# Two transformer layers and a scan block on one core: per-head 64-row products from compact operands in the second layer, and five modulation rounds moved from the first feed-forward into it

## The chip, the cores and the metric

The kernel runs on one core of a Trainium2 chip. The metric is the device time of one execution in microseconds (us); lower is better. Three executions of the kernel before gave 3799.74, 3799.99 and 3803.73 us, so the median is 3799.99 us.

## The reference, cut to what matters

512 latent tokens and 256 context tokens of width 1024 pass through two layers and then a third block. Every layer begins with a modulation: six vectors of 1024 values computed from a condition vector, used as shift, scale and gate.

```python
mod = silu(c) @ w_mod[l] + b_mod[l]          # 6 x 1024, for latent and for context
x = x + gate1 * mixer(norm(x) * (1 + scale1) + shift1)
x = x + gate2 * ffn(norm(x) * (1 + scale2) + shift2)
```

Layer 0 mixes by attention. Layer 1 ("odd") mixes by a neighbourhood attention and by a two-directional scan (RWKV-7) over 8 heads of 64:

```python
def step(S, inp):                            # S: 64 x 64 for each head, state of the scan
    sa = einsum('bhvk,bhk->bhv', S, kk_t)
    S = S * w_t - sa[..., None] * (kk_t * a_t) + v_t[..., None] * k_t
    return S, einsum('bhvk,bhk->bhv', S, r_t)
```

The scan runs over the context first, forward and backward; its end states start the scans over the latent tokens. The third block ("layer 2") has its own modulation `mod[2]`.

## The kernel before, in words

Everything is feature-major: 128 features on the partitions, tokens along the row. A large product is three matmuls for each pair of blocks (high and low halves of weights and activations), written by `mm3` (L361). A weight tile of 512 KB comes through a ring of three buffers (tag `wraw`), is rounded by ScalarE (`whi`, L321), and its remainder is taken by GpSimd (`wlo`, L322), each with two buffers.

**Modulation.** `mods(s, bias, rounds, dst)` (L367 to L392) computes one third of the six vectors in each round. A round has 8 steps; each loads two raw tiles of 512 KB (`mraw`, L377) and issues four matmuls of 32 output rows on four column strips (`psmod`, L380; the trace has two instructions for each of these float32 matmuls, so 8 in a step). At the end of a round the row is copied and transposed (`psmt`, L387). The steps are drawn one at a time by a generator, so other code can lay them between its own. In layer 0's feed-forward (`ffn`, called by `layer0`) all six rounds of `wm1` and `wm2` are drawn: 8 steps before the norm and 40 inside the loop over hidden blocks. Their raw tiles use the same ring of three buffers as the weights.

**The scan in chunks of 64.** Phase 1 (`rw_phase1`) computes for each pair of heads j (0 to 3) and direction d the operands of the chunked scan: `mix` makes k, v and r from the projection (`psz`, 24 matmuls each, then GpSimd L869 and VectorE L870, L871), `rw_pair` normalises, and `rw_dir` makes decays `E` and the operands `az` and `BKn`. `az` holds a pair of heads in a zero-padded layout: head e's 64 partitions are filled only in block e, so that a product over 128 rows gives both heads side by side.

```python
s.az = [pi.tile([128, s.nar, 2, n], F32, name=f"az{i}") for i in range(2)]
nc.tensor.matmul(ps[:, c * w:c * w + w], BKn[:, g + c]..., az[:, :, :, (g + c) * 64:(g + c) * 64 + 64])
```

The result `psA` (L1004) is masked by VectorE into `M` (L1006), multiplied with v (L1011) and copied out by ScalarE (L1012); operands go to DRAM. `rw_tri` inverts small triangular blocks on VectorE (`trisolve`, L792 and L794) and writes them to the DRAM tensors `dZ`, `dZT` in 16 transfers (L1041), half from the queue of SyncE (SP), half from that of ScalarE. Phase 2 (`rw_phase2`, `rw_unit`) loads these operands by unit (L1052 to L1066) and runs the chain of the scan.

**Order.** In `layer1` phase 1 of the context runs beside the projections of the neighbourhood attention; then phase 1 of the latent tokens runs with `rw_tri` and phase 2 of the context as its side work; then the neighbourhood attention with `rw_tri` of the latent; then phase 2 of the latent. A scheduler of the framework turns the program order into an order for each engine; each engine and each DMA queue then runs its own list strictly in order.

Of the kernel before, what the change touches and what calls it, by code (L numbers as in the profile page):

```python
# [8 lines left out]
F32 = mybir.dt.float32  # L9
# [3 lines left out]
ALU = mybir.AluOpType  # L13
# [230 lines left out]
class Base:  # L244
# [467 lines left out]
    def layer0(self):  # L712
# [33 lines left out]
        self.side = chain(self.mods(1, "bm1", (0, 1, 2), self.mod[1]), self.mods(2, "bm2", (0, 1, 2), self.mod[2]))  # L746
# [20 lines left out]
class K1:  # L767
# [74 lines left out]
    def rw_phase1(self, s):  # L842
# [4 lines left out]
        with ExitStack() as es:  # L847
# [7 lines left out]
            s.az = [pi.tile([128, s.nar, 2, n], F32, name=f"az{i}") for i in range(2)]  # L855
            s.vu = [pi.tile([128, s.nch, 128], F32, name=f"vu{i}") for i in range(2)]
            for z in s.az + s.vu:
                nc.gpsimd.memset(z, 0.0)
# [89 lines left out]
    def rw_dir(self, s, d, j, tp):  # L948
# [34 lines left out]
        for e in range(2):  # L983
            p = slice(64 * e, 64 * e + 64)
            if s.lat:
                nc.gpsimd.tensor_tensor(ch(az[p, 1, e]), ch(r[p]), E[p, :, i0:i0 + 64], op=ALU.mult)
                nc.sync.dma_start(s.dR[d][p, j], az[p, 1, e])
            nc.vector.tensor_tensor(ch(az[p, 0, e]), ch(kk[p]), E[p, :, iprev:iprev + 64], op=ALU.mult)
            nc.sync.dma_start(s.dAf[d][p, j], az[p, 0, e])
# [5 lines left out]
        w = nar * 128  # L995
        per = 512 // w
        mk = self.b(f"mar{d}")[:, :w].unsqueeze(1).to_broadcast([128, per, w])
        hc = max(per, nch // 2)
        for g in range(0, nch, per):
            if g % hc == 0:  # L1000
                M = tp.tile([128, hc, nar, 2, 64], F32, tag=f"M{d}", name="M", bufs=1)
            ps = s.psv("psA")
            for c in range(per):
                nc.tensor.matmul(ps[:, c * w:c * w + w], BKn[:, g + c].rearrange("p s t -> p (s t)"), az[:, :, :, (g + c) * 64:(g + c) * 64 + 64],  # L1004
                                 start=True, stop=True)
            nc.vector.tensor_tensor(M[:, g % hc:g % hc + per].rearrange("p c s e t -> p c (s e t)"), ps.rearrange("p (c x) -> p c x", c=per), mk, op=ALU.mult)  # L1006
            yield
            for c in range(g, g + per):
                for e in range(2):
                    o = ((c - g) // 2) * 128 + e * 64  # L1010
                    nc.tensor.matmul(ps[64 * (c % 2):64 * (c % 2) + 64, o:o + 64], M[:, c % hc, 0, e], vu[:, c, e * 64:e * 64 + 64], start=True, stop=True)  # L1011
            nc.scalar.activation(t2[:, g * 64:(g + per) * 64], ps[:, :per * 64], AF.Copy)  # L1012
            if (g + per) % hc == 0:
                g0 = g + per - hc
                for c in range(2):
                    nc.sync.dma_start(s.dA[d][:, c, g0 // 2:(g0 + hc) // 2, j].rearrange("p b e t -> p b (e t)"), M[0:64, c::2, 0].rearrange("p b e t -> p b (e t)"))
                if s.lat:
                    nc.sync.dma_start(s.dRR[d][:, j, g0:g0 + hc], M[:, :, 1].rearrange("p c e t -> p c (e t)"))
# [4 lines left out]
            yield  # L1023
        nc.sync.dma_start(s.dBV[d][:, j].rearrange("p b v -> p (b v)"), t2)

    def rw_tri(self, s):
        nc = self.nc
        Lq = 8 * s.nb
        with self.pool(name="tri", bufs=1, side="left") as trp, self.pool(name="trips", bufs=1, space=PSUM, side="right") as tps:
# [7 lines left out]
            for d in range(2):  # L1037
                for z, dst in ((Zs[d], s.dZ[d]), (ZTs[d], s.dZT[d])):
                    for p in range(4):
                        sl = slice(32 * p, 32 * p + 32)  # L1040
                        (nc.sync, nc.scalar)[d].dma_start(dst[sl, :, sl].rearrange("i u j -> u i j"), z[Lq * p:Lq * p + Lq])  # L1041
# [289 lines left out]
    def layer1(self):  # L1331
# [3 lines left out]
        with self.pool(name="psd1a", bufs=2, space=PSUM) as pA, self.pool(name="psd1d", bufs=3, space=PSUM) as pD, self.pool(name="psd1b", bufs=3, space=PSUM) as pB:  # L1335
# [4 lines left out]
            gF = self.gain("nffn1", m, 0, 4, "g1F")  # L1340
# [15 lines left out]
            st_c.side, st_c.bq, st_c.bc, st_c.bl, st_c.bk = "right", 2, 2, 1, 1  # L1356
# [10 lines left out]
        with self.pool(name="psd1c", bufs=2, space=PSUM) as pA, self.pool(name="psd1f", bufs=2, space=PSUM) as pD:  # L1367
# [849 lines left out]
```

## Time and profile before

| | before |
|---|---|
| median of three executions | 3799.99 us (3799.74 to 3803.73) |
| the profiled execution: its own time | 3793.68 us |
| its span from first to last instruction | 3791.9 us |
| TensorE (PE) busy | 3377.0 us (89%) |
| VectorE (DVE) busy | 1701.5 us (45%) |
| GpSimd (POOL) busy | 1402.0 us (37%) |
| ScalarE (ACT) busy | 1308.5 us (35%) |
| mean granted TensorE clock | 0.945 of 2.4 GHz |

Shares over the whole span hide the stages. The stages are read from windows: 515 to 1117 us is layer 0's feed-forward, 1117 to 1265 us phase 1 of the context, 1265 to 1592 us phase 1 of the latent tokens with the context's phase 2 beside it, 1592 to 1707 us the neighbourhood attention, and then the latent's phase 2.

### The profile page before, as it was taken

The numbers are of one execution on the slowest core, as the hardware profiler recorded it, in microseconds if no ns is written. First come the engines' busy times: TensorE is split into PE (matmuls) and PEld (weight loads), VectorE is DVE, ScalarE is ACT, GpSimd is POOL, SyncE is SP. The second block draws the span as 40 slices with busy tenths as digits, with TensorE's granted clock in tenths as the row PEclk, the third lists the DMA queues.
The fourth block names the chain that finished last, engine by engine and source line by source line (L and its number), as shares of the span: only waits on it lengthen the run. The fifth ranks groups of instructions, "written<-read, shape, count | busy, mean of one in ns | idle before, by whom it ended". The sixth has DMA issues, their size and how long they took to land. (4 is left out here: it accounts for less than half of the span.)

```text
span 3791.9 us, 49466 instructions
## 1 busy us (share of the span) xinstructions
PE 3377.0 (89%) x18772; PEld 2652.6 (70%) x18772; DVE 1701.5 (45%) x3170; ACT 1308.5 (35%) x2263; POOL 1402.0 (37%) x940
## 2 busy tenths in 40 slices
PE   7989989999999768888889989997898698789997
PEld 3679868787878546667768877666777457658885
DVE  4566231111124596574554426447657767431112
ACT  3366231121224433332234432333545323232222
POOL 1453222222223453321335544434544343244442
PEclk9999999999999878999889999998999899999999
DMA  6420243434334434636423433433455668512221
GB/s 230 164 106 7 88 151 117 150 116 141 126 106 129 111 111 140 175 88 204 146 70 124 131 105 95 122 93 99 140 155 155 158 193 247 164 61 95 95 97 65
DMA packets 397757, 480.78 MB, mean 127 GB/s; under 512 B 148432, under 2 KB 288656, under 8 KB 396496
## 3 DMA queue, kind: packets, MB, share of 16 engines
q1 hardware_dynamic: 384976, 476.05, 40.6%
q10 hardware_dynamic: 12544, 1.57, 0.3%
q8 instruction: 149, 2.44, 0.3%
q14 instruction: 88, 0.72, 0.1%
HBM read 391.86 MB, written 85.66 MB: 126 GB/s over the span
## 5 line engine op out<-in xcount | busy, mean ns | idle before, releaser
L322 POOL TENSOR_TENSOR wlo<-wraw,whi 128x1024 fp32r<-128x1024 f32 (+2 forms) x371 | 867.1, 2339 | 1512.7 <-ACT whi L321 1345.3
L321 ACT ACTIVATE whi<-wraw 128x1024 fp32r<-128x1024 f32 (+2 forms) x371 | 380.2, 1026 | 1041.3 <-issue 240.8
L504 DVE TENSOR_TENSOR pu<-pu,sg 128x512 f32<-128x512 f32 x88 | 55.6, 632 | 606.9 <-PE pu L361 554.2
L361 PE MATMUL pd<-hidh,wlo 128*128 128x512 f32 (+1 forms) x704 | 262.0, 372 | 9.2 <-POOL wlo L322 8.9
L361 PE MATMUL pd<-hidh,whi 128*128 128x512 f32 (+1 forms) x704 | 263.4, 374 | 6.1 <-ACT whi L321 3.8
L361 PE MATMUL pd<-hidl,whi 128*128 128x512 f32 (+1 forms) x704 | 260.5, 370 | 0.2 <-DVE hidl L506 0.2
L361 PE MATMUL pg<-hil,whi 128*128 128x512 f32 x528 | 214.3, 406 | 28.8 <-ACT hil L449 15.4
L361 PE MATMUL pg<-hil,wlo 128*128 128x512 f32 x528 | 211.4, 400 | 8.1 <-POOL wlo L322 7.1
L361 PE MATMUL pu<-hil,whi 128*128 128x512 f32 x528 | 209.7, 397 | 5.8 <-ACT whi L321 5.8
L361 PE MATMUL pu<-hil,wlo 128*128 128x512 f32 x528 | 209.2, 396 | 6.0 <-POOL wlo L322 6.0
L361 PE MATMUL pg<-lol,whi 128*128 128x512 f32 x528 | 210.5, 399 | 2.5 <-DVE lol L450 2.4
L361 PE MATMUL pu<-lol,whi 128*128 128x512 f32 x528 | 208.9, 396 | 0.0
L361 PE MATMUL psp<-hil,whi 128*128 128x512 f32 x416 | 174.0, 418 | 25.6 <-DVE yo L1782 11.8
L361 PE MATMUL psp<-lol,whi 128*128 128x512 f32 x416 | 171.0, 411 | 2.9 <-DVE lol L450 2.9
L361 PE MATMUL psp<-hil,wlo 128*128 128x512 f32 x416 | 170.3, 409 | 1.9 <-POOL wlo L322 1.8
L513 DVE SCALAR_TENSOR_TENSOR xT<-pd,mod,xT 128x512 f32<-128x512 f32 x80 | 59.8, 749 | 244.6 <-PE pd L361 244.6
L361 PEld LDWEIGHTS pd<-hidh,whi 128*128 128x128 f32 x704 | 133.3, 189 | 46.8 <-issue 15.1
L361 PEld LDWEIGHTS pd<-hidh,wlo 128*128 128x128 f32 x704 | 133.4, 189 | 39.1 <-POOL wlo L322 15.4
L361 PEld LDWEIGHTS pg<-hil,whi 128*128 128x128 f32 x528 | 101.5, 192 | 71.8 <-ACT hil L449 18.6
L361 PEld LDWEIGHTS pd<-hidl,whi 128*128 128x128 f32 x704 | 133.3, 189 | 24.0 <-issue 0.9
L792 DVE TENSOR_TENSOR Tl<-Al,Zl 64x31 f32<-64x31 f32 (+15 forms) x248 | 145.2, 585 | 4.1
L1574 DVE SCALAR_TENSOR_TENSOR psp<-xpl,vecs,psp 128x512 f32<-128x512 f32 x144 | 107.8, 751 | 84.5 <-ACT psp L1570 58.1
(588 smaller groups left out, 8145.9 us busy)
## 6 DMA issues: line engine op xcount, KB each, us to landing
mraw<-in_wm_dram SPq DMA_DIRECT2D x144, 512.0 KB, 4.3
wraw<-in_w2c_dram SPq DMA_DIRECT2D x72, 512.0 KB, 3.3
wraw<-in_wf0in_dram SPq DMA_DIRECT2D x44, 512.0 KB, 3.6
wraw<-in_wf1in_dram SPq DMA_DIRECT2D x44, 512.0 KB, 3.6
Z<-dZ SPq DMA_DIRECT2D x48, 256.0 KB, 3.8
ZT<-dZT SPq DMA_DIRECT2D x48, 256.0 KB, 4.1
wraw<-in_w1d_dram SPq DMA_DIRECT2D x23, 512.0 KB, 3.9
wraw<-in_wf2g_dram SPq DMA_DIRECT2D x22, 512.0 KB, 3.2
```

The source lines that it names most:

```text
L321: self.nc.scalar.activation(hi[:, :nk], t[:, :nk], AF.Copy)
L322: self.nc.gpsimd.tensor_tensor(lo[:, :nk], t[:, :nk], hi[:, :nk].bitcast(F32), op=ALU.subtract)
L361: nc.tensor.matmul(ps, l, r, start=first and i == 0 and p == 0, stop=last and i == n - 1 and p == 2)
L504: nc.vector.tensor_tensor(u, u, sg[:, :n], op=ALU.mult)
L513: nc.vector.scalar_tensor_tensor(x[:, j], pd[:, :n], gv[:, j:j + 1], x[:, j], op0=ALU.mult, op1=ALU.add)
L792: nc.vector.tensor_tensor(tmp, A[:L, rows, t:t + 1].to_broadcast([L, nr, ncl]), Z[:L, t:t + 1, cols].to_broadcast([L, nr, ncl]), op=ALU.mult)
L1574: nc.vector.scalar_tensor_tensor(pv, xp[:, :, t:t + L], w(t), pv, op0=ALU.mult, op1=ALU.add)
```

## The change

Of the six rounds of `wm1` and `wm2`, only the first stays in layer 0's feed-forward. The other five (40 steps) are drawn once per round of `rw_phase1` of the latent tokens, with a PSUM bank and a small pool of their own; what is left is drawn at the end. The gain vector `g1F` is computed later. `az` becomes compact, 128 partitions without zero blocks, filled in one instruction and stored with one transfer where there were two; the product is taken per head over 64 rows into two PSUM banks of four chunks each, and the mask is applied to each. The bank counts change: 2 to 3 for phase 1 of the latent, 2 and 2 to 1 and 1 for phase 2 of the context. The 16 `dZ` transfers all go to SP's queue. Phase 1 gets a further yield per group, and phase 2 of the context is drawn twice per round from round 13 on.

```diff
         self.mpools = self.psd, self.tp, (self.wp, "wraw", 3)
-        self.side = chain(self.mods(1, "bm1", (0, 1, 2), self.mod[1]), self.mods(2, "bm2", (0, 1, 2), self.mod[2]))
+        self.side = self.mods(1, "bm1", (0,), self.mod[1])
...
-            s.az = [pi.tile([128, s.nar, 2, n], F32, name=f"az{i}") for i in range(2)]
+            s.az = [pi.tile([128, s.nar, n], F32, name=f"az{i}") for i in range(2)]
...
-            for z in s.az + s.vu:
+            for z in s.vu:
                 nc.gpsimd.memset(z, 0.0)
...
-        for e in range(2):
-            p = slice(64 * e, 64 * e + 64)
-            if s.lat:
-                nc.gpsimd.tensor_tensor(ch(az[p, 1, e]), ch(r[p]), E[p, :, i0:i0 + 64], op=ALU.mult)
-                nc.sync.dma_start(s.dR[d][p, j], az[p, 1, e])
-            nc.vector.tensor_tensor(ch(az[p, 0, e]), ch(kk[p]), E[p, :, iprev:iprev + 64], op=ALU.mult)
-            nc.sync.dma_start(s.dAf[d][p, j], az[p, 0, e])
+        if s.lat:
+            nc.gpsimd.tensor_tensor(ch(az[:, 1]), ch(r), E[:, :, i0:i0 + 64], op=ALU.mult)
+            nc.sync.dma_start(s.dR[d][:, j], az[:, 1])
+        nc.vector.tensor_tensor(ch(az[:, 0]), ch(kk), E[:, :, iprev:iprev + 64], op=ALU.mult)
+        nc.sync.dma_start(s.dAf[d][:, j], az[:, 0])
...
-        w = nar * 128
-        per = 512 // w
+        w = nar * 64
+        per = 4
...
-            ps = s.psv("psA")
+            pa = [s.psv("psA") for e in range(2)]
             for c in range(per):
-                nc.tensor.matmul(ps[:, c * w:c * w + w], BKn[:, g + c].rearrange("p s t -> p (s t)"), az[:, :, :, (g + c) * 64:(g + c) * 64 + 64],
-                                 start=True, stop=True)
-            nc.vector.tensor_tensor(M[:, g % hc:g % hc + per].rearrange("p c s e t -> p c (s e t)"), ps.rearrange("p (c x) -> p c x", c=per), mk, op=ALU.mult)
+                for e in range(2):
+                    p = slice(64 * e, 64 * e + 64)
+                    nc.tensor.matmul(pa[e][:, c * w:c * w + w], BKn[p, g + c].rearrange("p s t -> p (s t)"), az[p, :, (g + c) * 64:(g + c) * 64 + 64],
+                                     start=True, stop=True)
+            for e in range(2):
+                nc.vector.tensor_tensor(M[:, :, :, e], pa[e][:, :per * w].rearrange("p (c s t) -> p c s t", c=per, t=64), mk, op=ALU.mult)
             yield
+            ps = pa[0]
...
             yield
+            if s.lat:
+                yield
...
-                        (nc.sync, nc.scalar)[d].dma_start(dst[sl, :, sl].rearrange("i u j -> u i j"), z[Lq * p:Lq * p + Lq])
+                        nc.sync.dma_start(dst[sl, :, sl].rearrange("i u j -> u i j"), z[Lq * p:Lq * p + Lq])
...
-            st_c.side, st_c.bq, st_c.bc, st_c.bl, st_c.bk = "right", 2, 2, 1, 1
+            st_c.side, st_c.bq, st_c.bc, st_c.bl, st_c.bk = "right", 1, 1, 1, 1
...
-        with self.pool(name="psd1c", bufs=2, space=PSUM) as pA, self.pool(name="psd1f", bufs=2, space=PSUM) as pD:
+        with self.pool(name="psd1c", bufs=2, space=PSUM) as pA, self.pool(name="psd1f", bufs=3, space=PSUM) as pD, \
+                self.pool(name="psd1m", bufs=1, space=PSUM) as pM, self.pool(name="mrow", bufs=1) as pR:
+            self.mpools = pM, pR, (self.wp, "wraw", 3)
+            mods = chain(self.mods(1, "bm1", (1, 2), m), self.mods(2, "bm2", (0, 1, 2), self.mod[2]))
...
             for i, _ in enumerate(self.rw_phase1(st_l)):
-                self.step(2 if i > 16 and i % 2 else 1)
+                self.step(2 if i > 12 else 1)
+                next(mods, None)
             self.drain()
+            for _ in mods:
+                pass
```

The order of instructions moves in three places. The first is SP's queue in layer 0's feed-forward. Before, every pair of weight loads (`wraw`) has a pair of modulation loads (`mraw`) beside it:

```order
L377 DMA mraw<-in_wm_dram 128x1024 x2
L315 DMA wraw<-in_wf0in_dram 128x1024 x2
L377 DMA mraw<-in_wm_dram 128x1024 x2
L315 DMA wraw<-in_wf0in_dram 128x1024 x2
L377 DMA mraw<-in_wm_dram 128x1024 x2
L315 DMA wraw<-in_wf0out_dram 128x1024
```

Now the weights stand alone there, up to the first loads of layer 1:

```order
L315 DMA wraw<-in_wf0in_dram 128x1024 x16
L315 DMA wraw<-in_wf0out_dram 128x1024 x8
L315 DMA wraw<-in_wf0in_dram 128x1024 x16
L315 DMA wraw<-in_wf0out_dram 128x1024 x8
L315 DMA wraw<-in_wf0in_dram 128x1024 x12
L315 DMA wraw<-in_wf0out_dram 128x768 x8
```

So the feed-forward loses 40 steps, and nothing takes their place. The second place is PE's list in phase 1 of the latent tokens, at the products `psA` of one head pair (j = 0). Before, they stand between projections `psz` of the next pair:

```order
L361 MATMUL psz<-hil,wlo 128x512
L1004 MATMUL psA<-az_10756,BKn 128x256 x2
L1004 MATMUL psA<-az_10757,BKn 128x256 x2
L361 MATMUL psz<-hil,whi 128x512
L361 MATMUL psz<-lol,whi 128x512
L361 MATMUL psz<-hil,wlo 128x512
```

Now they have half the columns, are twice as many, and modulation matmuls stand before and between them:

```order
L361 MATMUL psz<-hil,wlo 128x512
L380 MATMUL psmod<-mraw,siluc 32x512 x4
L1002 MATMUL psA<-az_10420,BKn 128x128
L1002 MATMUL psA<-az_10421,BKn 128x128 x4
L380 MATMUL psmod<-mraw,siluc 32x512 x2
L1011 MATMUL psA<-vu_10422,M 64x64
L380 MATMUL psmod<-mraw,siluc 32x512 x2
L1002 MATMUL psA<-az_10421,BKn 128x128 x4
L1011 MATMUL psA<-vu_10422,M 64x64 x8
L361 MATMUL psz<-hil,whi 128x512
```

The steps moved into gaps that the scheduler saw around `psA`; the 40 steps stand in 58 such rows. The third place is the end of the neighbourhood attention, where `rw_tri` of the latent stores its blocks. On SP's queue before (the other eight stand on ScalarE's):

```order
L1041 DMA dZ_1507<-Zl 32x32x32 x4
L1041 DMA dZT_1509<-Al 32x32x32 x4
L1052 DMA Z<-dZ_1507 128x512
L1294 DMA dno_9442<-no 128x512
L1053 DMA ZT<-dZT_1509 128x512
```

and now:

```order
L1041 DMA dZ_1507<-Zl 32x32x32 x4
L1041 DMA dZT_1509<-Al 32x32x32 x4
L1041 DMA dZ_1508<-Zl 32x32x32 x4
L1041 DMA dZT_1510<-Al 32x32x32 x4
L1294 DMA dno_9068<-no 128x512
L1052 DMA Z<-dZ_1507 128x512
L1053 DMA ZT<-dZT_1509 128x512
```

The first loads of phase 2 now stand behind all 16 stores, and ScalarE's list has none.

## Rows read from the trace of the kernel before

**Rows 1.** Windows by stage: width, busy time of engines (instructions), granted clock, DMA share, GB/s.

```profile
515.00:1117.00 602.00, 597.70 (x3461) 489.22 (x3459) 85.00 (x157) 109.39 (x158) 156.01 (x68) 1.00 0.38 128
1117.00:1265.00 148.00, 127.89 (x787) 107.85 (x788) 77.82 (x131) 77.50 (x139) 60.40 (x43) 0.96 0.41 129
1265.00:1592.00 327.00, 248.13 (x1355) 182.93 (x1356) 222.25 (x386) 111.00 (x190) 131.49 (x93) 0.83 0.47 133
```

**Rows 2.** PE's waits in 515:1117: who waited for whom, total us, times, longest.

```profile
PE pd L361 <- POOL wlo L322: 2.7, 5, 0.8
```

**Rows 3.** Windows, instructions on tile psmod, then psmt: PE, PEld, DVE.

```profile
515.00:1117.00 602.00, 41.55 (x312) 6.14 (x312) 3.46 (x5) 1.00 0.38 128
...
515.00:1117.00 602.00, 2.99 (x20) 2.30 (x20) 1.28 (x10) 1.00 0.38 128
```

**Rows 4.** PE's timeline around one step: start, length, instructions, idle before.

```profile
559.52 1.07 PE L380 MATMUL psmod<-mraw,siluc 128*32 128x512 f32 x8
560.52 0.50 PE L361 MATMUL pg<-hil,whi 128*128 128x512 f32 x1
```

**Rows 5.** PE's waits in 1265:1592, the longest total.

```profile
PE psA L1004 <- DVE BKn L992: 40.7, 7, 11.1
```

**Rows 6.** Timelines of DVE, POOL and PE in one such wait.

```profile
1337.19 0.68 DVE L988 TENSOR_TENSOR az<-kk,E 64x512 f32<-64x512 f32 x1
...
1342.36 2.24 DVE L988 TENSOR_TENSOR az<-kk,E 64x512 f32<-64x512 f32 x1
...
1348.42 2.05 PE L1004 MATMUL psA<-az,BKn 128*128 128x256 f32 x4 [9.90 <-DVE BKn L992]
```

**Rows 7.** Groups by line and shape in 1265:1592: busy us, mean ns.

```profile
L988 DVE TENSOR_TENSOR az<-kk,E 64x512 f32<-64x512 f32 x16 | 19.2, 1199 | 0.2
...
L986 POOL TENSOR_TENSOR az<-r,E 64x512 f32<-64x512 f32 x16 | 24.6, 1538 | 11.3 <-ACT E L976 10.5
...
L858 POOL MEMSET az<- 128x2048 f32 x2 | 3.5, 1805 | 0.0
```

**Rows 8.** PE's timeline at the start of the latent's phase 1.

```profile
1304.16 0.76 PE L361 MATMUL psz<-hil,whi 128*128 128x512 f32 x1 [12.12 <-DVE tw L871]
```

**Rows 9.** ACT's timeline at the end of the context's `rw_tri`.

```profile
1462.73 0.69 ACT L961 ACTIVATE t<-psa,small 128x512 f32<-128x512 f32 x1 [4.91 <-DMA dZT<-Al]
```

**Rows 10.** Timelines of ACT, SP and PE at the end of the latent's `rw_tri`.

```profile
1706.18 0.60 ACT L1276 ACTIVATE ptile<-pt 128x512 f32<-128x512 f32 x1 [9.46 <-DMA dZT<-Al]
...
1692.56 4.00 SPq L1041 DMA_DIRECT2D dZ<-Zl  x4
1696.66 8.31 SPq L1041 DMA_DIRECT2D dZT<-Al  x4
...
1710.45 0.32 SPq L1053 DMA_DIRECT2D ZT<-dZT  x1
...
1713.86 2.04 PE L1070 MATMUL p<-ZT,U 128*128 128x128 f32 x8 [5.06 <-DMA U<-rwl]
```

**Rows 11.** SP's timeline in layer 2, first and last of 16 such stores from one queue.

```profile
2981.80 2.98 SPq L1735 DMA_DIRECT2D dZ<-Zl  x4
...
2992.42 3.74 SPq L1735 DMA_DIRECT2D dZT<-Al  x4
```

**Rows 12.** PE's timeline, 128-column and 256-column float32 products at full clock.

```profile
1558.71 0.61 PE L1123 MATMUL psc<-UV,bk 128*128 128x128 f32 x4
1559.16 1.46 PE L1004 MATMUL psA<-az,BKn 128*128 128x256 f32 x6
```

**Rows 13.** PE's timeline in a unit of the context's phase 2.

```profile
1542.99 0.66 PE L1093 MATMUL p<-Z,at 128*64 128x128 f32 x8 [1.72 <-DVE at L1088]
```

**Rows 14.** Tile mraw in 76:260 (layer 0's projections): idle time that its users spent.

```profile
DMA mraw<-in_wm_dram: 6.7, 4
```

**Rows 15.** SP's timeline, twelve modulation loads in a row through three buffers.

```profile
468.56 24.08 SPq L377 DMA_DIRECT2D mraw<-in_wm_dram  x12
```

**Rows 16.** Windows as in rows 1, one wait for `BKn`.

```profile
1340.00:1360.00 20.00, 3.93 (x8) 2.35 (x8) 19.81 (x23) 2.58 (x4) 16.20 (x9) 0.56 0.41 125
```

More of the change, by code (lines that the diff above doesn't have):

```diff
@@ L993, in rw_dir @@
         yield
-        w = nar * 128
-        per = 512 // w
-        mk = self.b(f"mar{d}")[:, :w].unsqueeze(1).to_broadcast([128, per, w])
-        hc = max(per, nch // 2)
+        w = nar * 64
+        per = 4
+        mk = self.b(f"mar{d}")[:, :2 * w].rearrange("p (s e t) -> p s e t", e=2, t=64)[:, :, 0].unsqueeze(1).to_broadcast([128, per, nar, 64])
         for g in range(0, nch, per):
-            if g % hc == 0:
-                M = tp.tile([128, hc, nar, 2, 64], F32, tag=f"M{d}", name="M", bufs=1)
-            ps = s.psv("psA")
+            M = tp.tile([128, per, nar, 2, 64], F32, tag=f"M{d}", name="M", bufs=1)
+            pa = [s.psv("psA") for e in range(2)]
             for c in range(per):
-                nc.tensor.matmul(ps[:, c * w:c * w + w], BKn[:, g + c].rearrange("p s t -> p (s t)"), az[:, :, :, (g + c) * 64:(g + c) * 64 + 64],
-                                 start=True, stop=True)
-            nc.vector.tensor_tensor(M[:, g % hc:g % hc + per].rearrange("p c s e t -> p c (s e t)"), ps.rearrange("p (c x) -> p c x", c=per), mk, op=ALU.mult)
+                for e in range(2):
[4 more added lines that the diff above has]
+                nc.vector.tensor_tensor(M[:, :, :, e], pa[e][:, :per * w].rearrange("p (c s t) -> p c s t", c=per, t=64), mk, op=ALU.mult)
             yield
+            ps = pa[0]
             for c in range(g, g + per):
@@ L1010, in rw_dir @@
                     o = ((c - g) // 2) * 128 + e * 64
-                    nc.tensor.matmul(ps[64 * (c % 2):64 * (c % 2) + 64, o:o + 64], M[:, c % hc, 0, e], vu[:, c, e * 64:e * 64 + 64], start=True, stop=True)
+                    nc.tensor.matmul(ps[64 * (c % 2):64 * (c % 2) + 64, o:o + 64], M[:, c - g, 0, e], vu[:, c, e * 64:e * 64 + 64], start=True, stop=True)
             nc.scalar.activation(t2[:, g * 64:(g + per) * 64], ps[:, :per * 64], AF.Copy)
[L1013 to L1018, printed above, removed]
+            for c in range(2):
+                nc.sync.dma_start(s.dA[d][:, c, g // 2:(g + per) // 2, j].rearrange("p b e t -> p b (e t)"), M[0:64, c::2, 0].rearrange("p b e t -> p b (e t)"))
+            if s.lat:
+                nc.sync.dma_start(s.dRR[d][:, j, g:g + per], M[:, :, 1].rearrange("p c e t -> p c (e t)"))
             if g == 0:
@@ L1023, in rw_dir @@
             yield
+            if s.lat:
+                yield
         nc.sync.dma_start(s.dBV[d][:, j].rearrange("p b v -> p (b v)"), t2)
@@ L1339, in layer1 @@
             gA = [self.gain("nmix1", m, v, 1, f"g1A{v}") for v in range(2)]
-            gF = self.gain("nffn1", m, 0, 4, "g1F")
             hl, hc = self.htiles(S, "l"), self.htiles(C, "c")
@@ L1396, in layer1 @@
             hl = self.htiles(S, "l")
+            gF = self.gain("nffn1", m, 0, 4, "g1F")
             self.norm(self.x, S, gF, m[:, 0, 24:32], hl)
```

## The prediction

> **What bounds the kernel now.** I read the windows by stage first, then PE's waits in the two stages that the change touches, then the timelines at single places. The chain of work that ended last is of no help here: the profile follows it back through the later part of the program only, and the change lies before that.
>
> In layer 0's feed-forward, 602 us long, PE is busy 597.7 us at a granted clock of 1.00, that is at 2.4 GHz throughout [rows 1]; the longest thing that PE waits for there is a weight remainder, 2.7 us in all [rows 2]. This stage is PE's own work laid end to end, so PE work that leaves it shortens it by its full length. In phase 1 of the latent tokens nothing is the bound throughout: of 327 us PE is busy 248.1, DVE 222.3, POOL 131.5, and the mean clock is 0.83 [rows 1]. PE is idle 79 us. The largest part is 40.7 us in seven waits of `psA` for the operand `BKn` from DVE [rows 5]. Inside such a wait DVE works without a pause (19.8 of 20 us busy), POOL works 16.2 us, PE 3.9 us, and PE's clock falls to a mean of 0.56, so to 1.2 GHz for most of it [rows 16]. DVE is slow there because of POOL: the same product `az` takes 0.68 us alone and 2.24 us while POOL runs [rows 6].
>
> **The change, part by part.**
>
> *Steps taken out of the feed-forward.* There are 312 `psmod` instructions in that window, so 39 steps, busy 41.55 us: 1.065 us a step [rows 3]. One step takes 1.07 us by the timeline, and the next product begins 1.00 us after it began [rows 4], so a step costs its length and no more. 40 steps leave: 40 x 1.065 = 42.6 us. The transposes of five rounds leave too, 2.99 us [rows 3]. Their loads were hidden there (no wait of PE for them), so taking them away brings nothing more. Sum: -45.6 us. I hold this for the surest term. What could take from it is that weights come too late once PE gets through them faster; the waits for their remainders, 2.7 us in 602 [rows 2], leave much room before that.
>
> *Steps put into phase 1 of the latent tokens.* The same 45.6 us of PE work, and what PE waits for their loads. For these waits there are two rows: none in the feed-forward, and in layer 0's projections, where the steps also lie between other work, 6.7 us over 14 steps, 0.5 us a step [rows 14]. I take the second, 20 us for 40 steps: 65 us in all. The idle time that can take them in is 79 us less what the terms below remove, some 60 us. But PE's list is fixed: a step covers a gap only if it stands in that gap. The steps stand around `psA`, where the gaps are, though behind the matmul that waits as often as ahead of it. I take somewhat over half as covered: +28 us. The bounds are 0 (all covered) and +65 (none).
>
> *The cleared operand.* Two clears of `az` for the latent tokens, 3.5 us on POOL [rows 7], stand straight ahead of the first `mix` sum, for which DVE and then PE wait 12.1 us [rows 8]. They go: -3.5 us, with nothing behind them that would take their place but the clears of `vu`.
>
> *Compact products.* DVE issues 8 `az` products where there were 16 of 1.2 us, POOL 8 where there were 16 of 1.54 us [rows 7]; twice the partitions cost nothing, as length goes by the row. That is 9.6 us of DVE and 12.3 us of POOL less, all in the stretches where PE waits for `BKn`, and each POOL product that goes also stops delaying DVE. Four head pairs with 3 us each on the path: -12 us, bounds 0 and -22 (both sums in full). Half of the stores of `az` go from SP's queue too; SP is not waited for there, so this counts as nothing.
>
> *Products over 64 rows.* No row before shows a product with 64 contracted rows. By the nearest rows, four instructions of 128 columns take 0.61 us, 0.15 each, and six of 256 columns 1.46 us, 0.24 each [rows 12]. A chunk costs 2 x 0.24 = 0.49 us before and 4 x 0.15 = 0.61 us after if the two heads follow each other, half of that if they run at once: over 64 chunks +8 us or -12 us. I take +1, near the first, since nothing in this trace shows the second, but under it, since a part of either lies in PE's idle time. The Trainium skill ("TensorE: Matmul & The Clock Gate", Part 3) says that matmuls in different row groups run at once. By that rule this term would be the -12 us, and the sum 13 us lower. The Trainium skill has a rule against the change as well ("TensorEngine Tiling (Array Packing)", Key Properties): going from one tiling of the array to another drains TensorE. The changed list goes between 128-row products, 64-row products and 32-column strips at some 110 places. The trace shows no hole at such a place: the product behind a step begins 1.00 us after the step's begin, inside the step's own 1.07 us [rows 4]; so by the trace the term is zero.
>
> *One PSUM bank each for the context's phase 2.* A bank is free again only when its reader is done, so in each of 8 units two products that ran ahead now follow a hop through DVE or ACT. Such a hop costs PE 1.7 us where it shows [rows 13]: at most 8 x 2 x 1.7 = 27 us, none if phase 1 fills it. Phase 1 has work of other pairs beside it nearly always: +4 us.
>
> *The store queue.* At the context's `rw_tri` ACT waits 4.9 us for its own stores before it can go on with phase 1 [rows 9]; that goes: -4 us. At the latent's end ACT is blocked 9.5 us, so the last part of the neighbourhood attention is late, and SP, which must store its result first, issues `ZT` only at 1710.45, although its own stores were done at 1704.97; PE begins phase 2 at 1713.86 [rows 10]. With all 16 on one queue: in layer 2 sixteen like them take 2981.80 to 2996.16, 14.4 us, on SP alone [rows 11]. From 1692.6 that ends at 1707.0, and with ACT free the result is no longer late, so `ZT` is issued about 3 us earlier: -3 us. The other bound is the rate of the last four here, 8.31 / 4 = 2.1 us each [rows 10]: 33 us for sixteen, so +18 us.
>
> *The clock.* Where steps fill gaps, PE's clock stays up. Half clock over the 20 us of one wait costs the products behind it a few us each time; I take -5 us over the stage, bounds 0 and -25 (a third of the stage, by its mean of 0.83, lies at half clock, and PE works in perhaps half of that).
>
> Sum: -45.6 + 28 - 3.5 - 12 + 1 + 4 - 4 - 3 - 5 = -40 us. The profiled execution took 3793.7 us by its own time, the median of three 3800.0, 6.3 us more. After: 3753.6 for an execution like the profiled one, 3760 us beside the median. 0.2% of this kernel, 7.6 us, is about what a measurement can tell from no change.
>
> **The rivals.**
>
> *Nothing is hidden.* The steps stand on PE where it was busy, as many behind the waiting matmul as in the gap, and the 65 us come out in full, so 37 us more than in the sum: 3797 us, no change. For it: PE is busy 76% of the stage already, and its list is fixed. Against: 79 us of idle time, and the waits for `BKn` get shorter. A half-way case gives 3778.
>
> *The ring of three raw buffers becomes the bound; slower.* In the stage 80 modulation tiles and 13 weight tiles pass the same three buffers, and a modulation tile is freed by PE, whose list stands still for up to 11 us at `psA` [rows 5]. A weight tile then comes late, and its split, `mix` and the next pair with it. Price: twelve loads through this ring took 24.1 us with PE free, 2.0 us a tile [rows 15], so 93 tiles need 187 us at best. It decides from 327 / 93 = 3.5 us a tile: at 4.2 us a tile the stage is 391 us, 64 longer, and the total 3800 - 45.6 - 3 + 64 = 3815. Against it: that takes twice the bare rate of the ring. SP's queue, in which these loads now stand ahead of the loads of phase 2, would show it.
>
> *All is hidden, and the chain gets shorter.* The steps fall into gaps at 5 us in all, the compact products bring 22, the clock 10: 3800 - 45.6 + 5 - 3.5 - 22 - 4 - 3 - 10 + 5 = 3722. For it: the waits for `BKn` are shortened by just the work that goes. Against: each such wait moves other work too.
>
> **How the numbers follow.** Forecast (stage 1265 to 1592 grows by up to 25 us): 0.6. Half-way to nothing hidden (about 3778): 0.14. Nothing hidden (3797): 0.08. Slower by the ring: 0.08. All hidden: 0.1. The predicted time is the likeliest, 3760 us. The range 3722 to 3797 reaches to the all-hidden case and to the case in which nothing is hidden; it leaves out the ring and some tail, under 2 in 10. Faster by over 0.2% (below 3792.4): all of the forecast, the half-way case and all hidden, 0.83. Within 0.2%: the case of nothing hidden, 0.08, with a little of the ring, 0.09. Slower: 0.08.
>
> **What would show it.** In the profile after, the feed-forward should be about 556 us from the same products, with PE still over 98% busy. The next stage should be 327 to 350 us long with PE busy near 290, a clock above 0.83, and waits of `psA` for `BKn` well below 40.7 us. The wait of 12.1 us at its start should be near 8.5. `az` products should be half as many at the same or a shorter mean. If PE's waits for `mraw` pass 20 us, or weights come late and POOL waits for `psmod` there, the ring is the cause. The prediction is wrong if the feed-forward falls by less than 40 us, or if the next stage grows by more than 40.

## The result, and the profile after

The changed kernel takes 3825.27 us (median of 4, 3817.8 to 3832.34) beside 3799.86 us for the kernel before: ratio 1.0067, 95% interval 1.0046 to 1.0087. I had forecast 3760, with 3722 to 3797 as the range: it is slower, and outside.

Windows by stage of the kernel after (busy time and instructions of PE, PEld, DVE, ACT, POOL; granted clock, DMA share, GB/s), as [rows 1]:

```profile
500.00:1058.00 558.00, 556.80 (x3175) 489.16 (x3176) 91.58 (x160) 115.42 (x170) 159.56 (x70) 0.99 0.21 65
1058.00:1206.00 148.00, 136.35 (x824) 114.80 (x824) 69.05 (x121) 70.22 (x127) 54.91 (x36) 0.93 0.40 124
1206.00:1620.00 414.00, 335.73 (x1844) 202.39 (x1840) 202.74 (x406) 115.71 (x184) 110.62 (x85) 0.86 0.66 201
```

The first feed-forward is short as forecast. The third row is the loss: phase 1 of the latent tokens takes 414 us where it took 327. PE is busy 88 us longer there and idle as long as before (78 us, 79 before): nothing of the steps seems to lie in the idle time. DMA share went from 0.47 to 0.66, and the rate from 133 to 201 GB/s.

The same stage, instructions on tile `psmod` alone (PE, PEld, DVE), as [rows 3]:

```profile
1206.00:1620.00 414.00, 82.31 (x316) 11.20 (x312) 3.44 (x5) 0.86 0.66 201
```

About the same number of instructions (312) cost 41.55 us in the feed-forward [rows 3]; here they cost twice that. PE's timeline shows why:

```profile
1307.05 1.06 PE L380 MATMUL psmod<-mraw,siluc 128*32 128x512 f32 x8
1308.05 1.16 PE L1002 MATMUL psA<-az,BKn 64*128 64x128 f32 x10
1309.14 1.05 PE L380 MATMUL psmod<-mraw,siluc 128*32 128x512 f32 x4
1310.12 0.33 PE L1011 MATMUL psA<-vu,M 128*64 128x64 f32 x2
1311.57 1.05 PE L380 MATMUL psmod<-mraw,siluc 128*32 128x512 f32 x4 [1.12 <-DMA mraw<-in_wm_dram]
```

A whole step (8 instructions, four column strips) takes 1.06 us; half a step takes 1.05. Here PE's list has other products between the matmuls on a step's first tile and those on its second, so most steps are paid twice.

What PE waits for in the stage (us, times, longest):

```profile
PE psmod L380 <- DMA mraw<-in_wm_dram: 23.0, 11, 10.2
PE psz L361 <- DVE tw L871: 8.2, 1, 8.2
PE psA L1002 <- DVE BKn L990: 6.3, 3, 3.6
PE psz L361 <- POOL wlo L322: 5.3, 5, 1.8
PE psz L361 <- ACT whi L321: 4.8, 2, 4.6
```

The waits for `BKn`, 40.7 us before [rows 5], are nearly gone, and the start wait is 8.2 us (forecast 8.5). In their place stand waits for raw tiles and late weights. On the queue of SP, the waits of the loads of the moved rounds (L377):

```profile
SPq L377 <- PE psmod L380: 81.8, 28, 10.2
...
SPq L377 <- DMA mraw<-in_wm_dram: 17.6, 8, 4.7
...
SPq L377 <- POOL wlo L322: 10.9, 6, 2.7
```

SP stands for 110 us at loads of modulation tiles (81.8, 17.6 and 10.9), and the scan's loads and stores stand behind them in its list. DMA issues in the stage (number, KB each, median us from issue to landing):

```profile
mraw<-in_wm_dram SPq DMA_DIRECT2D x76, 512.0 KB, 4.4
wraw<-in_w1d_dram SPq DMA_DIRECT2D x12, 512.0 KB, 5.0
rwl<-az SPq DMA_DIRECT2D x16, 256.0 KB, 4.9
...
rwl<-t SPq DMA_DIRECT2D x8, 256.0 KB, 5.1
```

Of the scan's own stores those of `az` and `t` land about twice as late as without these loads (2.6 and 2.5 us in the run with one pair loaded, below); others hardly change (`BK`, 512 KB: 3.5 beside 3.3). One place where an engine then stands is a wait of ACT, two times in the stage:

```profile
ACT t L961 <- DMA rwl<-t: 19.2, 2, 11.3
```

That profile could be read as the ring rival come true: stage 414 us (rival 391), total 3825 (rival 3815), waits for `mraw` over 20 us. The experiments say otherwise.

### The profile page after: what moved, and what is told of

It is laid out like the page before. It is cut to its first block, busy times and chain, and to the rows that moved or that the text cites. A ratio compares the mean times of both kernels' runs of the same rounds, so it can differ in the third digit from the quotient of the medians.

```text
span 3823.1 us, 49641 instructions
## 1 busy us (share of the span) xinstructions
PE 3429.0 (90%) x18964; PEld 2675.8 (70%) x18964; DVE 1674.1 (44%) x3162; ACT 1308.0 (34%) x2248; POOL 1381.5 (36%) x928
## 5 line engine op out<-in xcount | busy, mean ns | idle before, releaser
L380 PE MATMUL psmod<-mraw,siluc 128*32 128x512 f32 x576 | 143.3, 655 | 39.1 <-DMA mraw<-in_wm_dram 36.2
```

The costliest lines, as they stand in the source:

```text
L380: nc.tensor.matmul(ps[32 * q:32 * q + 32], co[:, k * 32:k * 32 + 32], ws[q // 2][:, (q % 2) * 512:(q % 2) * 512 + 512], start=k == 0, stop ...
```

## The experiments

The theories are named A, B and C in the first expectation, and B1 to B3 in that of the own ring. Two lengths are compared throughout, read where a tile's products begin: the *stage*, from the first latent `psz` to the first product of the neighbourhood attention, and the *span*, from that `psz` to the readout of the scan (work can move over the seam between). The last columns are PE's time on `psmod` in the stage and the MB that modulation loads bring there (loads times their size). Stage and span come from one profiled execution of each run; the two profiles of the same kernel, *two rounds, spread* and *again*, differ by 8.6 us in the stage and 8.8 in the span, so smaller differences say little.

| run | ratio, 95% interval | psz begins | stage | span | psmod | MB |
|---|---|---|---|---|---|---|
| before | 1 | 1265.2 | 327.1 | 595.2 | 0 | 0 |
| after | 1.0067 (1.0046 to 1.0087) | 1207.7 | 413.2 | 679.6 | 82.2 | 42 |
| no move | 1.0002 (0.9984 to 1.0020) | 1271.6 | 339.8 | 592.3 | 0 | 0 |
| move only | 1.0100 (1.0085 to 1.0116) | 1197.6 | 440.7 | 712.9 | 83.8 | 42 |
| halves together | 1.0030 (1.0017 to 1.0042) | 1208.4 | 404.9 | 673.3 | 53.2 | 42 |
| one pair loaded | 0.9867 (0.9853 to 0.9882) | 1206.2 | 345.3 | 612.9 | 46.6 | 1 |
| own ring | 1.0083 (1.0064 to 1.0102) | 1208.7 | 427.0 | 695.4 | 92.4 | 42 |
| loads, few matmuls | 1.0065 (1.0050 to 1.0080) | 1207.7 | 415.4 | 681.1 | 24.0 | 42 |
| half-size loads | 0.9950 (0.9935 to 0.9965) | 1209.3 | 365.1 | 632.6 | 78.5 | 21 |
| compact only | 0.9994 (0.9984 to 1.0005) | 1270.1 | 332.1 | 587.1 | 0 | 0 |
| loads unread | 1.0008 (0.9995 to 1.0020) | 1208.0 | 384.5 | 654.3 | 44.4 | 42 |
| small loads, few matmuls | 0.9896 (0.9881 to 0.9911) | 1208.6 | 345.3 | 612.7 | 19.2 | 10 |
| own ring, loads by ACT | 1.0045 (1.0029 to 1.0062) | 1208.5 | 405.0 | 676.6 | 94.5 | 42 |
| two rounds, spread | 0.9979 (0.9964 to 0.9994) | 1250.4 | 337.6 | 602.5 | 28.7 | 17 |
| two rounds, dense | 0.9978 (0.9968 to 0.9987) | 1247.0 | 338.8 | 605.8 | 31.7 | 17 |
| two, spread, together | 0.9983 (0.9972 to 0.9994) | 1251.7 | 340.5 | 609.3 | 26.7 | 17 |
| three rounds, spread | 1.0004 (0.9993 to 1.0015) | 1234.6 | 361.2 | 627.2 | 49.4 | 25 |
| move only, two rounds | 0.9990 (0.9981 to 0.9998) | 1240.7 | 348.1 | 613.8 | 30.9 | 17 |
| two rounds, spread, again | 0.9974 (0.9963 to 0.9986) | 1246.6 | 346.2 | 611.3 | 29.3 | 17 |

### Which part of the change, and is it PE or the loads?

**No move.**

```diff
-        self.side = self.mods(1, "bm1", (0,), self.mod[1])
+        self.side = chain(self.mods(1, "bm1", (0, 1, 2), self.mod[1]), self.mods(2, "bm2", (0, 1, 2), self.mod[2]))
...
-            mods = chain(self.mods(1, "bm1", (1, 2), m), self.mods(2, "bm2", (0, 1, 2), self.mod[2]))
+            mods = iter(())
```

> The changed kernel with the five modulation rounds put back into the first feed-forward; compact operands, 64-row products, banks and queues stay as changed. Three theories. A, price of a step: in phase 1 of the latent tokens the four matmuls of a step stand as two separate pairs on PE (82 us for 40 steps in the trace of after, against 41.6 us in the feed-forward before) and nothing of it is hidden. B, the ring of three raw buffers and SP's queue hold up the stage. C, the rest of the change (64-row products, banks, extra yields) lengthens it. By A and B the rest of the change is a gain of about the size I forecast (-3.5 -12 +1 +4 -4 -3 = -17.5 us): stage 310 us, total 3775 to 3790. By C the stage is longer than the 327 us of before and the total 3805 or more.

No gain and no loss: ratio 1.0002, between the forecasts of the theories. So the rest of the change is not what costs, but it isn't the gain of 17.5 us either.

**Move only.** The kernel before, with the loop of the latent phase 1 drawing `next(mods, None)` as in the change.

> The kernel before with the five rounds moved alone (one PSUM bank for them, taken from the context's phase 2, which keeps two for its products and one for its chain). By A and B the move costs all of the loss and more: first feed-forward 46 us shorter, next stage 85 to 105 us longer, total 3840 to 3860. By C the move alone is the gain I forecast: total 3770 to 3785.

3842.06 us: C falls, A and B stand. On the padded operands the span grows by 118 us over before, on the compact ones by 84.

**Halves together.**

```diff
-                for q in range(4):
-                    nc.tensor.matmul(ps[32 * q:32 * q + 32], co[:, k * 32:k * 32 + 32],
...
+                mul(2)
+                with self.tc.issue_after(mul(3).ins):
+                    mul(0)
+                    mul(1)
```

> The changed kernel with one edit: the two matmuls on a step's first raw tile must follow the two on its second tile on PE, so that all four stand together; loads, ring and queue stay. By A the 160 matmuls take 42 to 45 us in the stage where they took 82, the stage shrinks by 35 to 40 us and the total is 3785 to 3790. By B a step now holds two of three ring buffers until the second tile has landed, PE's waits for mraw grow beyond the 23 us, and the total stays at 3815 to 3850 although PE's time on the steps falls. C says nothing of it.

Tile `psmod` in its stage:

```profile
1208.40:1613.30 404.90, 53.22 (x312) 7.02 (x312) 3.44 (x5) 0.81 0.65 206
```

The function `mul(q)` issues the matmul of strip q, so strips 0 and 1 come only behind strip 3. PE gets back 29 us, the span 6, the total 10.5 (3814.73). Theory A, that the doubled price is the loss, explains a small part only.

**One pair loaded.**

```diff
+                    if self.once is None:
+                        self.once = wp.tile([128, 2, 1024], F32, name="mraw")
+                        nc.sync.dma_start(self.once, src[:2].rearrange("h p a b -> p h (a b)"))
+                    ws = [self.once[:, 0], self.once[:, 1]]
...
```

> The changed kernel with the 80 modulation loads of the latent phase 1 left out: one pair of tiles is loaded once and used by all 40 steps, so that the modulation values of five rounds are not the reference's. PE's steps stay, the ring has the 13 weight tiles alone. By A the stage keeps PE's work on the steps, 42 to 60 us according to how many stand together, and is 370 to 390 us long, total 3780 to 3800. By B it also loses the waits for mraw, late weights and late scan loads: stage 340 us or less, total 3750 or less.

Windows of its stage, then two rows of its DMA issues:

```profile
1206.20:1551.50 345.30, 298.39 (x1864) 203.14 (x1865) 207.41 (x404) 114.13 (x183) 128.50 (x85) 0.87 0.44 129
```

```profile
rwl<-az SPq DMA_DIRECT2D x16, 256.0 KB, 2.6
...
rwl<-t SPq DMA_DIRECT2D x8, 256.0 KB, 2.5
```

3752.32 us, 47 under before. All 40 steps are still on PE (46.6 us and 3 of transposes), and the span grows by 20.6 us over the run without the move: 58% of that work is hidden. The hiding that I forecast works; the loads undo it.

### What about the loads?

**Own ring.**

```diff
-self.mpools = pM, pR, (self.wp, "wraw", 3)
+self.mpools = pM, pR, (pR, "mraw", 3)
```

> The changed kernel with a ring of three buffers of their own for the modulation tiles of the latent phase 1 (the 13 weight tiles keep the three that they had before). What is open after the first four runs is which property of the loads costs the 68 us by which the stage is longer (413 us, from the first latent psz to the first product of the neighbourhood attention) than with one pair loaded once (345 us). B1, the ring: 93 tiles pass three buffers at 4.4 us a tile, and weights and steps wait for a buffer. B2, the bytes: 42 MB more in the stage make every transfer slower (az stores land in 4.9 us where they took 2.3). B3, the list of SP: a load that waits for PE to free its buffer holds the scan's loads and stores behind it. By B1, with twice the buffers: stage 350 to 375 us, total 3760 to 3790. By B2: stage 405 to 420, total 3815 to 3830. By B3 the steps still free their buffers late and SP still stands: stage 395 to 415, total 3805 to 3830.

427 us, 3830.62: twice the buffers don't help at all, although PE's waits for raw tiles fall from 23.0 us to 7.7:

```profile
PE psmod L380 <- DMA mraw<-in_wm_dram: 7.7, 8, 1.8
```

The ring is not the bound, and the rival's mechanism falls although its number was close. The stage is even longer than any of the three theories had it; its 14 us over the changed kernel stay unexplained.

**Loads, few matmuls.** Of 40 steps 35 read 16 columns of each tile.

> The changed kernel with all 80 loads of the moved rounds, but only the first step of each round with its full matmuls; the other 35 steps read 16 columns of each of their two tiles, to free it. So five rounds of modulation are not the reference's. PE's work on the steps falls from 82 us to about 20. By A (it is PE's work that lengthens the stage) the stage shrinks by 60 us to about 350, total 3760. By B, in any of its three forms, loads and ring stay: by B1 a buffer's cycle loses only the 1 to 2 us of the matmuls, stage 385 to 405, total 3795 to 3815; by B2 the same or more.

```profile
1207.70:1623.10 415.40, 305.20 (x1704) 220.70 (x1705) 202.35 (x404) 113.94 (x181) 110.47 (x82) 0.75 0.64 201
```

With 58 us less of PE's work on the steps the stage is as long as in the changed kernel, and PE just idles 110 us of it. The granted clock is lower (0.75, 0.86 in the changed kernel) and PE's other work takes 28 us longer (281 against 253), so this run doesn't price the steps; but taking most of PE's work on them away shortens nothing while the loads stay. A is out.

**Half-size loads.**

```diff
-                    nc.sync.dma_start(t, src[(r * KC + k) * 2 + hf])
+                    half = pp is not self.psd
+                    nc.sync.dma_start(t[:, :4 if half else 8], src[(r * KC + k) * 2 + hf][:, :4 if half else 8])
...
```

> The changed kernel with the same 80 loads, ring and steps, but each load of the moved rounds brings half of its tile (256 KB), and the matmuls read that half twice, so five rounds of modulation are not the reference's. 21 MB less in the stage. By B2 the stage loses half of the 68 us or more: 350 to 380 us, total 3760 to 3790. By B1 and B3 a tile's cycle through the ring (3 x 4.4 = 13 us) loses only the shorter landing, 1 to 2 us: stage 385 to 405, total 3795 to 3815.

3777.41 us, stage 365, with `psmod` still at 78.5 us and every load and buffer in place: bytes. SP's waits at the loads for PE's release get shorter with them (53.9 us, 81.8 in the changed kernel).

**Loads unread.** The run with one pair, and the 80 loads issued beside it into the shared ring.

> One pair of modulation tiles is loaded once and used by all 40 steps, as in the run that came out 47 us under before, and the 80 loads are issued all the same, into the shared ring of three at the same places, but nothing reads them. So five rounds of modulation are not the reference's. The bytes are those of the changed kernel; no load waits for PE and no step for a load. By B2 (the bytes slow every other transfer) the stage is 385 us or more and the total 3795 or more. If the loss needs the loop between them (PE's list waits for a load, the next load waits in SP's list for PE, the scan's transfers wait behind it), the stage stays at 345 to 365 and the total at 3752 to 3775.

```profile
1208.00:1592.50 384.50, 304.88 (x1848) 204.81 (x1848) 209.20 (x403) 113.89 (x181) 112.17 (x82) 0.84 0.70 218
```

Bytes that nobody reads cost 41 us of span (654.3 against 612.9). The other 25 (679.6 against 654.3) come only where steps read the loads and hold their buffers. By the medians the two parts are 48 and 25 us. The 41 are not landing times alone: SP still stands 55 us at these loads, 36.2 for the landing of an earlier one in the ring and 19.2 for GpSimd, which frees the weights' buffers:

```profile
SPq L381 <- DMA mraw<-in_wm_dram: 36.2, 18, 3.6
```

**Small loads, few matmuls.** As *loads, few matmuls*, but 64 KB in place of 512 KB for those 35 steps.

> As the run in which 35 of 40 steps read only 16 columns of their tiles (stage 415 us, total 3821), but the loads of those 35 steps bring 64 KB each in place of 512 KB. Ring, SP's list, number of loads and waits for PE stay; 32 MB less. By B2 the stage falls to 330 to 355 us, total 3735 to 3765. By the loop (B1, B3) it loses the shorter landing only, about 2 us of the 13 us that a buffer's cycle takes: stage 365 to 400, total 3775 to 3805.

```profile
1208.60:1553.90 345.30, 279.70 (x1703) 206.45 (x1703) 206.98 (x404) 114.13 (x182) 114.28 (x84) 0.84 0.51 150
```

Same list, same number of loads, and each still waits for PE's release: 32 MB less shorten the span by 68 us. The span is that of the run with one pair loaded (612.7, 612.9), with SP standing at PE's release half as long as with whole loads (71.4 us there):

```profile
SPq L378 <- PE psmod L383: 36.1, 27, 5.2
```

So the loop costs little without the bytes behind it.

**Own ring, loads by ACT.** `nc.scalar.dma_start` for the moved rounds.

> The changed kernel with a ring of three buffers of their own for the moved rounds (that alone left the stage at 427 us), and their loads issued by ACT in place of SP. SP's list then holds no load that waits for PE; ACT's does. Same bytes. By B2 the stage stays at 410 to 435 us, total 3810 to 3835. By B3, SP's list alone, the stage falls to 350 to 385, total 3760 to 3795, if ACT's own waits for the buffers don't take its place.

3815.86 us, 15 under the own ring with SP. A store of `az` lands in 2.8 us here and in 4.6 with the loads on its own queue:

```profile
mraw<-in_wm_dram ACTq DMA_DIRECT2D x80, 512.0 KB, 4.8
...
rwl<-az SPq DMA_DIRECT2D x16, 256.0 KB, 2.8
...
rwl<-t SPq DMA_DIRECT2D x8, 256.0 KB, 5.1
```

The Trainium skill ("DMA: Bandwidth & Descriptors", Queues, rings and completion order) says that each DMA engine takes the queues that have work in turn; by that rule a store on another queue than the loads isn't behind them. The row of `az` agrees; the others don't show it (`t` 5.1 us, 4.7 with the loads on SP; `M` of 256 KB 3.9 and 3.0; `vu` 4.8 and 3.2). The stage is 22 us shorter than with the own ring and SP, but now ACT stands at the loads: its waits that end with a `psmod` product sum to 43.5 us.

### Where does the price begin?

**Two rounds, spread.** Rounds 1 and 2 of `mod[1]` are moved, the other three stay.

```diff
+if i % 3 == 0:
     next(mods, None)
```

> The changed kernel with two of the five rounds moved (the rest of the second table's first part), a step at every third place of the stage in place of every place, and three rounds left in the first feed-forward. 32 loads, 17 MB in the stage. The feed-forward gains 17 to 18 us against the run without the move (3797.6). If the price of the loads goes by their bytes or number (86 us for 80 loads), the stage grows by 34 us and the total is 3810 to 3818. If the stage's transfers can take in 17 MB beside its own without a wait, it grows by the unhidden part of PE's 17 us, 5 to 10 us, and the total is 3783 to 3792: faster than both kernels.

```profile
1250.40:1588.00 337.60, 277.03 (x1635) 191.49 (x1635) 202.57 (x392) 112.99 (x181) 121.07 (x84) 0.86 0.60 177
```

3790.24 us, ratio 0.9979 (0.9964 to 0.9994): within the second forecast.

**Two rounds, dense.** The same without the `if`.

> Two rounds moved, as in the spread run (3790 us), but a step at every place of the stage, so that the 16 steps and their 32 loads stand in the first 16 of its 44 places. Same bytes, same PE work. If what costs is how densely the loads stand among the scan's transfers, the stretch loses what the changed kernel loses there, 32/80 of the 66 us that loads cost it (41 for the bytes, 25 for the waits between loads and steps), 26 us: total 3805 to 3818. If what costs is only bytes beyond what the stage has room for, the total is that of the spread run, 3786 to 3796.

3790.51 us: density isn't what costs.

**Two, spread, together.**

> Two rounds moved and spread over the stage, and the four matmuls of a step forced together on PE (they took 28.7 us for 15 steps, 1.9 us a step, where four together take 1.05). 10 to 12 us of PE work less. If PE's work on the steps is hidden where loads are few, nothing changes: 3787 to 3793. If it shows, the total falls by up to 10 us: 3780 to 3786.

3792.02 us: no gain. But `psmod` takes 26.7 us, not 18, so the edit took 2 us from PE and not 10: in six of the 15 steps that the trace holds, the last matmul still stands apart, behind other products, and several rows run at half the clock (1.9 us where 1.06 is usual, granted clock 0.50). What the whole 10 us would bring isn't shown.

**Three rounds, spread.**

> Three rounds moved (two of the second table, one of the third), a step at every second place: 48 loads, 25 MB. The feed-forward gains 12 to 13 us more than with two rounds. If the stage can still take the loads in between its own transfers, the total is 3778 to 3786. If the price rises with the bytes as the half-size loads showed (21 MB in 80 loads: stage 365 us against 345), the gain is given back: 3788 to 3800.

3800.99 us, just above the second forecast, ratio 1.0004: the third round gives back what the three gain.

**Move only, two rounds.**

> The kernel before with two rounds moved and spread, and nothing else of the change (one PSUM bank for the steps from the chain of the context's phase 2). If the gain of the spread run (7.6 us) is the move's, this run has it as well: 3788 to 3794. If the compact products are what makes room, 3796 or more.

3793.89 us, ratio 0.9990 (0.9981 to 0.9998): at the edge of the first forecast. On the padded operands the gain is about 4 us by the ratio, half of the spread run's; the two intervals overlap, so whether the compact products make room isn't shown.

**Two rounds, spread, again.**

> The run with two rounds moved and spread once more, in five rounds, since its interval (0.9964 to 0.9994) ended at the bound of what can be told. If its gain stands: ratio 0.997 to 0.999, total 3786 to 3794.

3790.95 beside 3801.84 us, ratio 0.9974 (0.9963 to 0.9986): with two rounds moved the program is faster than both kernels, spread or dense (0.9978).

Over the run without the move, the start of the latent `psz` comes 20 to 25 us earlier with two rounds, 37 with three, 64 with five: some 12 us a round. The span grows by 10 to 19 us with two, 35 with three, 87 with five: the first two cost 5 to 10 us each, the third about 20 (16 to 25, by which of the runs with two it is set beside), the last two 26 each. The move pays up to two rounds.

### And the compact products?

**Compact only.** The kernel before with the edits of `rw_dir` and the operand's tile; rounds, step pattern and yields as before. Not as before, though the expectation says so, are the stores of `rw_tri`: all 16 stay on SP's queue, as in the change, so this run doesn't take the store queue out.

> The kernel before with the compact operands and 64-row products alone (and the operand's clearing gone); rounds, step pattern, yields, the two store queues and two PSUM banks for the products of the context's phase 2 as before, with the bank for the second head's products taken from its chain. The run without the move came out at the time of before, where I had forecast 17.5 us less. If the loss lay in the banks, the extra yields or the one store queue, this one gives the -14 us forecast for the compact products and the clearing: total 3780 to 3790. If the compact products themselves give nothing (the wait for BKn is then behind other work on DVE), the total is 3795 to 3805.

Ratio 0.9994 (0.9984 to 1.0005). PE's waits, then DVE's timeline ahead of one of them:

```profile
PE psA L1002 <- DVE BKn L990: 37.5, 6, 11.4
```

```profile
1346.84 2.43 DVE L792 TENSOR_TENSOR Tl<-Al,Zl 64x175 f32<-64x175 f32 x1
1349.19 0.15 DVE L980 COPY PLl<-E 128x8 f32<-128x8 f32 x1
1349.26 0.68 DVE L986 TENSOR_TENSOR az<-kk,E 128x512 f32<-128x512 f32 x1
1349.87 0.33 DVE L792 TENSOR_TENSOR Tl<-Al,Zl 64x175 f32<-64x175 f32 x1
1350.12 0.68 DVE L989 SCALAR_TENSOR_TENSOR BKn<-t,t 128x512 f32<-128x512 f32 x1
1350.72 0.57 DVE L794 TENSOR_TENSOR Zl<-Zl,Tl 64x175 f32<-64x175 f32 x2
```

DVE is busy 17 us less in the stage (204.9 against 222.1), and the wait for `BKn` is 3 us shorter than before [rows 5]; `psA` now waits 6.8 us for `PLl` and 6.5 for `M`, also from DVE, where it waited 1.4 for `M` before. Between the links of the chain to `BKn` stand steps of the triangular solve (`Tl`, `Zl`). That these are what the wait now consists of is read from the list, not tested.

## Why the prediction was wrong, point by point

- **Steps taken out, -45.6.** Mis-sized, in my disfavour: from the first product to the last, the feed-forward takes 558.4 us after and 617.4 in the run without the move, 59.0 less. I priced the steps by their own busy time (44.5 us with transposes). PE's busy time fell by 54 (610.6 to 556.7), and its idle time by 5: products beside a step run longer too (mean of the first `pg` group 414 ns with steps, 397 without). I had put the rule of the Trainium skill ("TensorEngine Tiling (Array Packing)", Key Properties), that a change of tiling drains TensorE, at zero by [rows 4]; some 14 us over 39 steps are in favour of it, though no run here singles it out.
- **Steps put in, +28.** This step failed: on the span the term is +87. Its first part held: of 50 us of PE work about 29 were hidden ("somewhat over half"), and 21 came out. The second part, "20 us for 40 steps" by [rows 14], took from a stage with other traffic what PE waits for a step's own tiles, and left out what 42 MB do to the stage's other transfers: 41 us for bytes that nobody reads and 25 more when steps read them, 66 in place of 20. The row was misread as well: of its 6.7 us PE itself waited 3.0, the rest was idle time of its weight loads. The warning stood in the trace before. The stage had a DMA share of 0.47 over 327 us [rows 1], 154 us. Twelve such loads took 24.1 us [rows 15], with the DMA engines busy 0.74 of that stretch (the last figure but one below), 1.5 us a load, so 80 take 119 us. An estimate from these two gives 273 of 327 us, a share of 0.83, before any chain of store, load and product has its say. The trace after shows the same 273 us (0.66 of 413), in a longer stage.

```profile
468.56:492.64 24.08, 20.80 (x72) 5.81 (x74) 12.99 (x15) 11.63 (x21) 0.00 (x0) 1.00 0.74 239
```

- **Steps cost 1.065 us each.** Wrong here: 2.1 a step, mostly since halves stand apart, and some rows run at half the clock (1.92 us). In the stage of [rows 14] that was to be seen already (14 steps, `psmod` busy 19.07 us, 1.36 a step); I took the price from the feed-forward alone. Yet with the halves together only 10.5 us came back, and with most matmuls left out nothing.
- **Compact products -12.** Nothing: the wait for `BKn` is 37.5 us where it was 40.7 [rows 5]. The work that went was not the last thing the wait hung on. One premise was misread: the `az` product of 0.68 us [rows 6] was not alone, POOL was busy 0.60 us of it, on `az` too; beside the one of 2.24 us POOL worked 1.69 us on `wlo`, which the change leaves in place. That fewer POOL products free DVE doesn't follow from these two rows.
- **Cleared operand -3.5.** Right: the start wait is 6.6 us without the move, 8.2 with it, 12.1 before [rows 8].
- **64-row products +1.** Near: in the stage PE takes 51.5 us for the products of before, and for those that replace them 50.3 with the compact operands alone, 48.9 without the move, 46.6 after. In the kernel after four such matmuls (8 instructions) take 1.16 us at 1312.55, and eight (16 instructions) take the same 1.16 at 1369.15. The rule of the Trainium skill ("TensorE: Matmul & The Clock Gate", Part 3), that products in different row groups run at once, fits the second; in the sums over the stage little of it shows.
- **One bank +4, store queue -7.** Not separated, since the run with the compact operands alone has the one queue too. The length of the 16 stores on SP came as forecast, 14.2 us (1716.18 to 1730.35 after; forecast 14.4 [rows 11]). Without the move all these together, with the products, came to nothing.
- **Clock -5.** The mean granted clock rose, 0.83 to 0.86; what that was worth was not separated.
- **The ring as a rival.** Right in place and nearly in size, wrong in mechanism: more buffers didn't help, fewer bytes did. The sign that I had set for it (waits for `mraw` over 20 us) came, 23.0 us, and proved nothing.

The account: -64 us at the start of the latent `psz` and +87 on the span, both over the run without the move, give +23 beside the +28 between the medians of the two runs. Against the forecast of -40 that is 13 us better at the steps taken out, 59 worse at the steps put in, and 17.5 worse at the rest, which came to nothing: 63 of the 65 us by which the total was missed. Open: how the 66 us of the loads split between transfers that land later and the list of SP that stands longer for them. Moving the loads to ACT made ACT stand in SP's place, and SP still stood 44 us at the stores of `rw_tri` (L1041), which the profile puts down to landings of `mraw`; so that run doesn't tell.

## What to carry to other kernels

When work moves into another stage, cost its loads as traffic of that stage, not only as waits of the work itself: add their transfer time to the share that the DMA engines are busy there, and treat the stage as full well before the sum reaches its length. By the estimate above the sum is 0.62 of the stage's 327 us with two rounds, which paid, 0.69 with three, whose third didn't, and 0.83 with five. Move by portions and look for the portion that stops paying; here two rounds of five paid. A rival whose number comes true isn't thereby shown: its own resource has to be widened once.

## What was not expected of the hardware

Two column strips of 32 cost what four cost (1.05 us for half a step, 1.06 for a whole one), so work that runs side by side in strips loses half its rate when a scheduler parts it. And 42 MB of loads that no instruction reads lengthened the span by 41 us, while the DMA engines were busy 0.70 of the time on average.
